# Output product by Strassen's algorithm over pairs of token blocks, in a mixer layer on one core

## The chip, the core and the metric

One core of a Trainium2 chip runs the whole layer in one launch. The metric is the device time of a run in microseconds (us); the time of a kernel is the median of its runs.

## What is computed

One layer of a mixer over 4096 tokens of width 1024, all in float32. The last product, `y @ W_out`, is the part that is changed.

```python
ada = cond @ w_ada[l] + b_ada[l]
shift, scale, gate = jnp.split(ada, 3, axis=-1)
h = _rms(x) * norm_gain[l]
h = h * (1.0 + scale[:, None, :]) + shift[:, None, :]
proj = h @ w_in[l]
q, k, v, g_attn, u, v_gm, g_gm = jnp.split(proj, splits, axis=-1)
attn = _windowed_gqa(q, k, v, q_gain[l], k_gain[l], sink[l])
gm = _chunked_gmlp(u, v_gm, w_s[l], b_s[l])
y = jnp.concatenate([attn * jax.nn.silu(g_attn), gm * jax.nn.silu(g_gm)], axis=-1)
x = x + gate[:, None, :] * (y @ w_out[l])
```

`x` is (1, 4096, 1024), `w_in` (1024, 2816), `w_out` (1024, 1024).

## The kernel before

The tokens are worked on in 32 blocks of 128 (`NB`), and widths in chunks of 128 (`KC` = 8). Every large product is made in three passes: each float32 operand is split into a high part (a cast to float32r on ACT) and a low part (the difference, on DVE or POOL), and high x high, high x low and low x high are added up in a bank of PSUM. So a group of 512 output columns over 1024 inputs takes 8 x 3 = 24 matmuls of 512 columns (`proj_ops`, L83).

There are three stages. The first makes q, k, v and the attention gate of each block and the windowed attention; the attention half of y goes to DRAM transposed (`yT[b][0]`). The second, the gMLP stage (loop at L905), makes v, g and u of each block (`gmlp_v`, `gmlp_gu`, `gmlp_u`; steps v and g of a block, block after block), 24 matmuls each, and after every four blocks the spatial mixing `gmlp_mix` (L839): 24 matmuls of 256 columns, evacuations on DVE, 16 transposes on PE, copies on ACT, and a store to `yT[b][1]`. In it, after blocks 8 to 17, the gate is made (`bg_gate`, `end_gate`).

The third stage makes the output. For each block `load3` (L958) loads the block of y and of x, `split3` (L966) splits y, and two groups of 24 matmuls follow, each evacuated by `out_block` (L976), which adds x on DVE and stores. The weights are loaded by `load_wo` (L882, multiplied by the gate on DVE or, for the last two rows, POOL) and split by `split_wo` (L887) from the last two blocks of the gMLP stage on; block 0 takes the weight rows one after the other as they are ready (loop at L985). Blocks 1 to 31 then run with all weights in SBUF (loop at L1002).

The pool `base` holds tiles over all stages, `hp` those of one stage (h2, then h3), `vr` (w2v) lies at the other end of SBUF and holds the weights of v and the buffers `raw2` (3). `y_tile` (L954) puts two of three blocks' operands into `base` and the third into the pool of the stage:

```python
    def y_tile(b, dt, tag, name):
        pool, bufs = (base, 2) if b % 3 < 2 else (hp, 1)
```

The Tile framework reorders instructions within an engine's queue by its own costs; every queue then runs in the order built. SP issues nearly all DMAs, in one queue.

Of the kernel before, what the change touches and what calls it, by code (L numbers as in the profile page):

```python
# [42 lines left out]
def body(tc, x, xT, c, cT, w_adaT, b_adaT, w_gate, b_gate, ngT, w_in, q_gain, k_gain, sink, wsT, bsT, w_out, out):  # L43
# [6 lines left out]
    yT = [[dram.tile([P, 4, P], F32, name=f"yT{b}_{h}") for h in range(2)] for b in range(NB)]  # L50

# [827 lines left out]
    woraw, woh2 = {}, []  # L879
    wo = [None] * KC  # L880

    def load_wo(k):  # L882
        woraw[k] = vr.tile([P, D], F32, tag="raw2", name=f"woraw{k}", bufs=3)
        nc.sync.dma_start(woraw[k], w_out[k * P : (k + 1) * P])
        (V if k < 6 else G).tensor_mul(woraw[k], woraw[k], gate)

    def split_wo(k):  # L887
        raw = woraw[k]
        if k < KC // 2:
            wo[k] = [[base.tile([P, 512], F32R, tag=f"{t}{2 * k + i}", name=f"wo{t}{k}_{i}") for i in range(2)] for t in "hl"]  # L890
        else:
            if not woh2:
                woh2.extend(halves("wo"))
            t = woh2[4 * k - 16 : 4 * k - 12]
            wo[k] = [t[:2], t[2:]]
        for i in range(2):
            r = raw[:, i * 512 : (i + 1) * 512]
            h, l = wo[k][0][i], wo[k][1][i]
            A.copy(h, r)
            V.tensor_tensor(l, r, h.bitcast(F32), ALU.subtract)  # L900
# [4 lines left out]
    for b0 in range(0, NB, NC):  # L905
# [19 lines left out]
        else:  # L925
            steps = [(n, b) for b in range(b0, b0 + NC) for n in "vg"]
        steps.append(("v", b0 + NC))
        for (n, b), (_, nb) in zip(steps[:-1], steps[1:]):
            if nb != b and nb < NB and (n, b) != ("u", 2):
                split2(nb)  # L930
            if n == "v":
                gmlp_v(b, vh, vl)
                continue
# [8 lines left out]
            if NB - 2 <= b:  # L942
                load_wo(b - (NB - 2))
# [6 lines left out]
    xp = p3.enter_context(tc.tile_pool(name="x3", bufs=4, reuse_waits="tile"))  # L950

    ld = {}

    def y_tile(b, dt, tag, name):  # L954
        pool, bufs = (base, 2) if b % 3 < 2 else (hp, 1)
        return pool.tile([P, KC, P], dt, tag=tag, name=f"{name}{b}", bufs=bufs)

    def load3(b):  # L958
        yr = y_tile(b, F32, "xraw", "yr")
        for h in range(2):  # L960
            nc.sync.dma_start(yr[:, 4 * h : 4 * h + 4], yT[b][h])
# [4 lines left out]
    def split3(b):  # L966
        yr, _ = ld[b]
        yh, yl = y_tile(b, F32R, "xh", "yh"), y_tile(b, F32R, "xl", "yl")
        A.copy(yh, yr)  # L969
        V.tensor_tensor(yl, yr, yh.bitcast(F32), ALU.subtract)  # L970
        return yh, yl

    woh = [[None] * KC for _ in range(2)]
    wol = [[None] * KC for _ in range(2)]

    def out_block(b, group, i):  # L976
        _, xt = ld[b]
        V.tensor_tensor(xt[:, i * 512 : (i + 1) * 512], group, xt[:, i * 512 : (i + 1) * 512], ALU.add)  # L978
        nc.sync.dma_start(out[b * P : (b + 1) * P, i * 512 : (i + 1) * 512], xt[:, i * 512 : (i + 1) * 512])

    NF = 1
    first = []
    for b in range(NF):
        load3(b)
    for k in range(KC):  # L985
        split_wo(k)
        if k + 2 < KC:
            load_wo(k + 2)
        for i in range(2):
            woh[i][k], wol[i][k] = wo[k][0][i], wo[k][1][i]  # L990
        if k == 0:
            for b in range(NF):
                yh, yl = split3(b)
                for i in range(2):
# [59 lines left out]
```

## Time and profile before

| | us |
|---|---|
| runs (3): median | 1760.36 |
| runs: lowest, highest | 1754.94, 1763.99 |
| profiled execution: its own time | 1755.96 |
| profiled execution: its span | 1754.2 |
| of it: first stage and start, to about | 860 |
| gMLP stage | 860 to 1391 |
| output stage | 1391 to 1754 |

The span runs from the first to the last instruction of one execution; 1.8 us lie around it. PE is TensorE's matmuls, PEld its weight loads, DVE VectorE, ACT ScalarE, POOL GpSimd, SP the engine that issues DMAs.

### The profile page before, as it was taken

How to read it: one execution, taken by the hardware profiler on the slowest of the kernel's cores; microseconds unless marked ns; L12 is line 12 of the kernel's file. 1: busy time of each engine (PE TensorE's matmuls, PEld its weight loads, DVE VectorE, ACT ScalarE, POOL GpSimd, SP SyncE). 2: the span in 40 equal slices, each digit the busy share in tenths (PEclk: the TensorE clock that was granted, in tenths of full speed). 3: DMA queues.
4: the chain of work that ended last, by engine and by line, in shares of the span. 5: the costliest groups of instructions: out<-in, count | busy, mean ns of one | idle time of the engine just before them, and what ended most of it. 6: DMA issues, size and time to landing. Idle time of an engine off the chain costs nothing.

```text
span 1754.2 us, 22761 instructions
## 1 busy us (share of the span) xinstructions
PE 1695.0 (97%) x8408; PEld 1405.0 (80%) x8408; DVE 988.4 (56%) x2143; ACT 689.8 (39%) x1505; POOL 522.7 (30%) x494
## 2 busy tenths in 40 slices
PE   6799999999999999998999999999999999999999
PEld 4578888888888888866778888888888788888887
DVE  7878787777888777779763332342333632222221
ACT  3476666666666666665511121212212310000000
POOL 5653334344333434356322222222232200000000
PEclk9899999999999999999999999999999999999999
DMA  7522221222221122123340111111111274444431
GB/s 261 186 84 72 73 67 48 68 73 73 73 73 61 49 72 91 37 66 109 98 151 27 59 50 36 49 38 59 49 36 49 85 231 144 143 145 144 143 131 60
DMA packets 61712, 156.24 MB, mean 89 GB/s; under 512 B 7584, under 2 KB 7584, under 8 KB 61600
## 3 DMA queue, kind: packets, MB, share of 16 engines
q1 hardware_dynamic: 56848, 146.13, 24.6%
q10 hardware_dynamic: 4752, 8.65, 1.3%
q8 instruction: 66, 1.08, 0.3%
q14 instruction: 46, 0.38, 0.1%
HBM read 121.20 MB, written 33.55 MB: 88 GB/s over the span
## 4 chain that ended last, share of the span: by engine, by line
PE 78%; DVE 10%; issue 2%; ACT 2%; POOL 1%; DMA 1%; SPq 0%; ACTq 0%; POOLq 0%; DVEq 0%
PE po L59 23%; PE pg L59 16%; PE pv L59 9%; PE pq L59 8%; PE pu L59 8%; PE pT L62 4%; PE s L59 4%; DVE y L598 2%; DVE pr L549 1%; PE sv L59 1%; PE pk L59 1%; DVE gf L493 1%; DVE qT L517 1%; ACT lo L596 1%; PE yT L62 1%
## 5 line engine op out<-in xcount | busy, mean ns | idle before, releaser
L95 POOL TENSOR_TENSOR xl<-xraw,xh 128x1024 fp32r<-128x1024 f32 x58 | 151.5, 2613 | 379.1 <-ACT xh L94 379.1
L569 POOL TENSOR_SCALAR pr<-pr,den 128x384 f32<-128x384 f32 (+1 forms) x256 | 147.2, 595 | 160.6 <-DVE vs L443 96.1
L978 DVE TENSOR_TENSOR xt<-po,xt 128x512 f32<-128x512 f32 x64 | 44.2, 691 | 254.2 <-PE po L59 251.4
L553 ACT ACTIVATE pr<-pr,mx 128x384 f32<-128x384 f32 (+1 forms) x256 | 153.8, 601 | 59.0 <-DVE mx L549 58.4
L59 PE MATMUL po<-wo,yh 128*128 128x512 f32 x512 | 158.9, 391 | 0.0
L549 DVE CUSTOM_DVE_ANT_0 pr<-s,negd,nsink 128x384 f32<-128x384 f32 (+1 forms) x256 | 152.2, 605 | 11.3 <-PE s L59 5.9
L578 ACT CAST ph<-pT 128x512 fp32r<-128x512 f32 x188 | 109.7, 585 | 116.5 <-PE po L59 44.2
L59 PE MATMUL pu<-w2u,xh 128*128 128x512 f32 x480 | 148.7, 391 | 0.0
L59 PE MATMUL s<-kT,qT 128*128 128x384 f32 (+1 forms) x512 | 135.6, 346 | 12.9 <-DVE mx L549 11.7
L969 ACT CAST yh<-yr 128x1024 fp32r<-128x1024 f32 x32 | 33.7, 1053 | 281.2 <-PE po L59 263.2
L579 DVE TENSOR_TENSOR pl<-pT,ph 128x512 fp32r<-128x512 f32 x188 | 125.9, 684 | 15.7 <-ACT ph L578 15.6
L62 PEld LDWEIGHTS pT<-ident,pr 128*128 128x128 f32 x752 | 93.6, 141 | 34.8 <-POOL pr L569 6.6
L62 PE MATMUL pT<-ident,pr 128*128 128x128 f32 x752 | 116.2, 274 | 5.2 <-DVE pl L579 3.4
L59 PEld LDWEIGHTS po<-wo,yh 128*128 128x128 f32 x512 | 96.3, 188 | 21.5 <-DVE wo L900 0.8
L59 PEld LDWEIGHTS s<-kT,qT 128*128 128x128 f32 x512 | 86.2, 188 | 33.5 <-DVE mx L549 20.6
L81 POOL TENSOR_TENSOR ssv<-ssv,mhalf 128x8 f32<-128x8 f32 x32 | 52.8, 1651 | 180.7 <-DVE ssv L80 180.5
L59 PEld LDWEIGHTS pu<-w2u,xh 128*128 128x128 f32 x480 | 90.8, 189 | 19.0
L94 ACT CAST xh<-xraw 128x1024 fp32r<-128x1024 f32 x61 | 64.1, 1051 | 101.4 <-PE pu L59 99.3
L59 PE MATMUL po<-woh,yh 128*128 128x512 f32 x256 | 100.3, 392 | 0.0
L59 PE MATMUL po<-wol,yh 128*128 128x512 f32 x256 | 100.2, 392 | 0.0
L59 PE MATMUL po<-wo,yl 128*128 128x512 f32 x256 | 100.1, 391 | 0.0
L59 PE MATMUL po<-woh,yl 128*128 128x512 f32 x256 | 100.0, 391 | 0.0
(288 smaller groups left out, 4302.0 us busy)
## 6 DMA issues: line engine op xcount, KB each, us to landing
xraw<-xT SPq DMA_DIRECT2D x61, 512.0 KB, 3.9
xtok<-x SPq DMA_DIRECT2D x32, 512.0 KB, 5.1
yr<-yT SPq DMA_DIRECT2D x64, 256.0 KB, 2.9
xt<-x SPq DMA_DIRECT2D x32, 512.0 KB, 4.7
out<-xt SPq DMA_DIRECT2D x64, 256.0 KB, 2.1
wada<-w_adaT SPq DMA_DIRECT2D x16, 512.0 KB, 5.6
yT<-ybuf ACTq DMA_DIRECT2D x32, 256.0 KB, 2.0
yT<-y SPq DMA_DIRECT2D x31, 256.0 KB, 5.2
```

What stands on the lines that cost most here:

```text
L59: pe(T.matmul(ps, lhsT, rhs, start=start, stop=stop))
L62: pe(T.transpose(ps, src, ident))
L81: G.tensor_tensor(dst, dst, mhalf[:, :width], ALU.pow)
L94: A.copy(xh, xr)
L95: ins = eng.tensor_tensor(xl, xr, xh.bitcast(F32), ALU.subtract)
L549: V.tensor_tensor_reduce(flat(t[:, s0:s1]), flat(pss[:, s0:s1]), flat(negd[:, b % 3, s0:s1]), -(2.0 ** -(h + 1)), nsink[:, h : h + 1], ALU ...
L553: A.activation(t, t, AF.Exp, bias=m[:, i : i + 1], scale=-1.0, accum_out=d["den", j][:, i : i + 1])
L569: G.tensor_scalar(t, t, den[:, i : i + 1], 1.0, ALU.mult, ALU.mult)
L578: A.copy(ph, pt)
L579: V.tensor_tensor(pl, pt, ph.bitcast(F32), ALU.subtract)
L598: V.tensor_tensor(d["y"][e * HD : (e + 1) * HD, 2 * j : 2 * j + 2], po[:HD, e::2], lo[:, e::2], ALU.add)
L978: V.tensor_tensor(xt[:, i * 512 : (i + 1) * 512], group, xt[:, i * 512 : (i + 1) * 512], ALU.add)
```

## The change

Two blocks of tokens are taken together. Their y is cut into four quarters A11, A12, A21, A22 (block i, half h of the 1024 inputs), the gated weights into B11, B12, B21, B22 (half of the inputs, half of the outputs). Seven products of halves take the place of eight, with four sums of quarters of y (S1 to S4, on POOL), four of the weights (T1 to T4, on DVE) and sums of the products, part of which PE makes by adding into the same bank (X, Y, Z). The weights and their sums are made once, in the gMLP stage (`wo_rows`, `wo_sums`, `wo_last`), stored in DRAM (`wB`), loaded again in pieces of 512 KB (`stage_w`) and split (`split_wm`): B11 and T2 into the place of v's weights, T3 and T1 into that of g's, the others when the output stage begins (`ready`). For this g of block 30 and v of block 31 change places. The first two products stand ahead of the last `gmlp_mix`.

```diff
+    wB = {m: dram.tile([P, KC // 2, 512], F32, name=f"wB_{m}") for m in ("B11", "T2", "T3", "T1", "B21", "B22", "T4")}
...
+    def wo_rows(k):
+        chunk["r"] = []
+        for kk in (k, k + KC // 2):
+            t = vr.tile([P, D], F32, tag="raw2", name=f"woraw{kk}", bufs=3)
+            nc.sync.dma_start(t, w_out[kk * P : (kk + 1) * P])
+            V.tensor_mul(t, t, gate)
...
+        V.tensor_tensor(t1, b12, b11, ALU.subtract)
+        V.tensor_tensor(t2, b22, t1, ALU.subtract)
+        V.tensor_tensor(b12, b22, b12, ALU.subtract)
+        for m, src in (("B11", b11), ("T1", t1), ("T2", t2), ("T3", b12), ("B21", b21), ("B22", b22)):
+            nc.sync.dma_start(wB[m][:, k], src)
...
+    ORDER = (("A11", "B11", "X"), ("S2", "T2", "Y"), ("S3", "T3", "Z"), ("S1", "T1", "Y"), ("A12", "B21", "X"),
+             ("S4", "B22", "Y"), ("A22", "T4", "Z"))
...
+    def split_wm(m, i, eng=None):
+        t = staged.pop((m, i))
+        for j in range(2):
+            h, l = (wts[m][a][2 * i + j] for a in range(2))
+            A.copy(h, t[:, j])
+            (eng or V).tensor_tensor(l, t[:, j], h.bitcast(F32), ALU.subtract)
...
+            G.tensor_tensor(sums3[n], q[a], q[b], op)
...
+    def prep3(p, i):
+        n = ORDER[i][0]
+        src = (quarters(p) | sums3)[n]
+        h, l = opnd[n]
+        A.copy(flat(h), src)
+        V.tensor_tensor(flat(l), src, flat(h).bitcast(F32), ALU.subtract)
...
+        for k in range(KC // 2):
+            for j, (l, r) in enumerate(((xh, wh), (xh, wl), (xl, wh))):
+                pe(T.matmul(ps, l[:, k], r[k], start=i < 3 and k == 0 and j == 0, stop=k == KC // 2 - 1 and j == 2,
+                            skip_group_check=i >= 3))
...
+        if i == 0:
+            A.copy(p1, banks["X"])
+        if i == 1:
+            V.tensor_tensor(u2, banks["Y"], p1, ALU.add)
+        if i == 3:
+            V.tensor_tensor(u4, banks["Y"], p1, ALU.add)
...
+        if i == 0:
+            G.tensor_tensor(x12, x12, part["p1"], ALU.add)
+        if i == 1:
+            G.tensor_tensor(x21, x21, part["u2"], ALU.add)
+        if i == 3:
+            G.tensor_tensor(x22, x22, ybuf[0], ALU.add)
...
+        if z:
+            V.tensor_tensor(dst, banks[z], dst, ALU.add)
...
+            nc.sync.dma_start(out[r0 : r0 + P, h * 512 : (h + 1) * 512], dst)
...
+            if b0 + NC == NB:
+                steps[5], steps[6] = steps[6], steps[5]
...
+    def ready(m):
         for i in range(2):
...
+            split_wm(m, i, (V, G)[i])
+            if pend:
+                stage_w(*pend.pop(0), hp, "stage", 3)
...
+            if p == 0:
+                if 1 <= i < 4:
+                    ready(late[i])
...
+            elif p + 1 < NP:
+                prep3(p + 1, i)
```

How the built order moves, at two places. PE, before, at the end of block 0 of the output stage (`po3_0_0`, `po3_0_1` are its two banks, `wo10` to `wo13` the high and low parts of the last weight row, `yh0`, `yl0` the split block):

```order
L59 MATMUL po3_0_0_13349<-wo10_13418,yh0_13345 128x512 [waits Activation_49]
L59 MATMUL po3_0_0_13349<-wo12_13420,yh0_13345 128x512 [waits DVE_49]
L59 MATMUL po3_0_0_13349<-wo10_13418,yl0_13346 128x512
L59 MATMUL po3_0_1_13350<-wo11_13419,yh0_13345 128x512 [waits Activation_49]
L59 MATMUL po3_0_1_13350<-wo13_13421,yh0_13345 128x512 [waits DVE_49]
L59 MATMUL po3_0_1_13350<-wo11_13419,yl0_13346 128x512
```

PE, now, in the first pair, behind the last transposes (`oX0`, `oY0`, `oZ0` are the banks of pair 0, `oX1` of pair 1; `woT1h`, `woT1l` are T1's parts, `wo0` to `wo5` B21's, `oxh1`, `oxl0`, `oA11` split operands):

```order
L967 MATMUL oY0_13428<-woT1l2_13407,oxh1_13410 128x512 [waits Pool_49]
L967 MATMUL oY0_13428<-woT1h2_13403,oxh1_13410 128x512
L967 MATMUL oY0_13428<-woT1h3_13404,oxh1_13410 128x512 [waits Activation_49]
L967 MATMUL oY0_13428<-woT1l3_13408,oxh1_13410 128x512 [waits Pool_49]
L967 MATMUL oY0_13428<-woT1h3_13404,oxh1_13410 128x512
L967 MATMUL oX0_13427<-wo0_13531,oxl0_13411 128x512 [waits Activation_49]
L967 MATMUL oX0_13427<-wo4_13535,oxl0_13411 128x512 [waits DVE_49]
L967 MATMUL oX0_13427<-wo0_13531,oxl0_13411 128x512
L967 MATMUL oX0_13427<-wo1_13532,oxl0_13411 128x512 [waits Activation_49]
L967 MATMUL oX0_13427<-wo4_13535,oxl0_13411 128x512 [waits DVE_49]
L967 MATMUL oX0_13427<-wo1_13532,oxl0_13411 128x512
L967 MATMUL oX1_13714<-wo3h0_13221,oA11_13250 128x512 [waits Activation_49]
```

PE now waits for POOL too, where the weights' low parts are split between DVE and POOL, and takes up pair 1 in the middle of pair 0.

POOL, before, its last work (the split and the norms of the last v blocks, then two weight rows; nothing follows):

```order
L95 TENSOR_TENSOR xl31_13103<-xraw31_13100,xh31_13102 128x1024 [waits DMAHW4_49,PE_49,Activation_49]
L81 TENSOR_TENSOR ssv30_13093<-ssv30_13093,mhalf_126 128x8 [waits DVE_49]
L81 TENSOR_TENSOR ssv31_13193<-ssv31_13193,mhalf_126 128x8 [waits DVE_49]
L885 TENSOR_TENSOR woraw6_13426<-woraw6_13426,gate_10659 128x1024 [waits DMAHW5_49,DMAHW7_49,DMAHW2_49,DVE_49]
L885 TENSOR_TENSOR woraw7_13439<-woraw7_13439,gate_10659 128x1024 [waits DMAHW6_49,DMAHW3_49,DVE_49]
```

POOL, now, from the second half of T1 on (`xt3_0` and `xt3_1` are x tiles, `s12` holds S1 and S2, `yr` and `yr3` are loaded blocks of y):

```order
L928 TENSOR_TENSOR woT1l2_13407<-stT1_1_13547,woT1h2_13403 128x512 [waits DMAHW4_49,PE_49,Activation_49]
L928 TENSOR_TENSOR woT1l3_13408<-stT1_1_13547,woT1h3_13404 128x512 [waits PE_49,Activation_49]
L984 TENSOR_TENSOR xt3_00_13526<-xt3_00_13526,p1_13253 128x512 [waits DMAHW6_49,DVE_49,PE_49]
L986 TENSOR_TENSOR xt3_01_13527<-xt3_01_13527,u2_13254 128x512 [waits DMAHW7_49]
L988 TENSOR_TENSOR xt3_01_13527<-xt3_01_13527,ybuf0_9850 128x512 [waits DVE_49]
L949 TENSOR_TENSOR S3_13389<-yr3_0_13524,yr3_1_13525 128x512 [waits DMAHW2_49,DMAHW0_49,Pool_49]
L949 TENSOR_TENSOR s12_13249<-yr3_1_13525 128x512 [waits DMAHW3_49]
L949 TENSOR_TENSOR s12_13249<-s12_13249,yr3_0_13524 128x512 [waits Pool_49]
L949 TENSOR_TENSOR S3_13389<-yr0_13237,yr1_13238 128x512 [waits DMAHW5_49,DVE_49]
L949 TENSOR_TENSOR S4_13390<-yr3_0_13524,s12_13249 128x512 [waits DMAHW1_49,Pool_49]
L928 TENSOR_TENSOR wo5_13536<-stB21_1_13568,wo2_13533 128x512 [waits DMAHW4_49,Activation_49]
L928 TENSOR_TENSOR wo5_13536<-stB21_1_13568,wo3_13534 128x512 [waits Activation_49]
```

POOL had no work in the output stage but for its start; now the additions to x, the sums of the next pairs and half of the weights' low parts stand in one queue.

## Rows read from the trace of the kernel before

**Rows 1.** The page, engine totals: busy us, share of the span, instructions.
```profile
PE 1695.0 (97%) x8408; PEld 1405.0 (80%) x8408; DVE 988.4 (56%) x2143; ACT 689.8 (39%) x1505; POOL 522.7 (30%) x494
```
**Rows 2.** Stages: us, busy PE, PEld, DVE, ACT, POOL, PEclk, DMA share, GB/s.
```profile
860.00:1391.00 531.00, 524.90 (x2410) 430.33 (x2409) 206.80 (x322) 110.41 (x159) 131.04 (x59) 1.00 0.17 59
1391.00:1410.00 19.00, 16.99 (x91) 13.40 (x90) 15.18 (x24) 8.34 (x15) 6.31 (x2) 1.00 0.52 174
1410.00:1750.00 340.00, 340.00 (x1489) 279.49 (x1488) 80.05 (x93) 31.59 (x30) 0.00 (x0) 1.00 0.42 141
```
**Rows 3.** The page, costliest groups: the output matmuls, count, busy us, mean ns.
```profile
L59 PE MATMUL po<-wo,yh 128*128 128x512 f32 x512 | 158.9, 391 | 0.0
...
L59 PE MATMUL po<-woh,yh 128*128 128x512 f32 x256 | 100.3, 392 | 0.0
L59 PE MATMUL po<-wol,yh 128*128 128x512 f32 x256 | 100.2, 392 | 0.0
L59 PE MATMUL po<-wo,yl 128*128 128x512 f32 x256 | 100.1, 391 | 0.0
L59 PE MATMUL po<-woh,yl 128*128 128x512 f32 x256 | 100.0, 391 | 0.0
```
**Rows 4.** The chain of waits, output stage: start us, us, what.
```profile
1402.59 1.01 PE yT L62 x8
...
1409.49 340.91 PE po L59 x1490
```
**Rows 5.** Timeline of PE, first matmuls of groups: start us, us, what.
```profile
1374.93 0.39 PE L59 MATMUL pv<-w2vh,xh 128*128 128x512 f32 x1
...
1380.53 0.39 PE L59 MATMUL pg<-w2gh,xh 128*128 128x512 f32 x1
...
1385.99 0.62 PE L59 MATMUL pu<-w2u,xh 128*128 128x512 f32 x2
...
1391.43 0.28 PE L59 MATMUL sv<-vh,wsh 128*128 128x256 f32 x1
...
1392.85 0.39 PE L59 MATMUL po<-woh,yh 128*128 128x512 f32 x1
```
**Rows 6.** Timeline of PE, first matmuls of output blocks 2, 3 and 4.
```profile
1420.96 0.40 PE L59 MATMUL po<-woh,yh 128*128 128x512 f32 x1
...
1432.12 0.39 PE L59 MATMUL po<-woh,yh 128*128 128x512 f32 x1
...
1443.00 0.39 PE L59 MATMUL po<-woh,yh 128*128 128x512 f32 x1
```
**Rows 7.** Groups by line and form: count | busy us, mean ns | idle before.
```profile
L777 POOL TENSOR_TENSOR w2vl<-w2rawv,w2vh 128x512 fp32r<-128x512 f32 x4 | 5.2, 1290 | 9.4 <-PE po L59 7.9 <-ACT w2vh L776 1.5
...
L900 DVE TENSOR_TENSOR wol<-woraw,woh 128x512 fp32r<-128x512 f32 x8 | 5.3, 685 | 0.6 <-ACT woh L899 0.6
...
L899 ACT CAST woh<-woraw 128x512 fp32r<-128x512 f32 x8 | 4.7, 618 | 6.1 <-PE pg L59 5.4 <-DVE woraw L885 0.6
```
**Rows 8.** Timelines of POOL and DVE, start of the output stage.
```profile
1396.75 2.39 POOL L885 TENSOR_TENSOR woraw<-woraw,gate 128x1024 f32<-128x1024 f32 x1 [10.62 <-DMA woraw<-w_out]
1403.14 3.92 POOL L885 TENSOR_TENSOR woraw<-woraw,gate 128x1024 f32<-128x1024 f32 x1 [4.00 <-DVE wo L900]
...
1397.87 1.81 DVE L900 TENSOR_TENSOR wo<-woraw,wo 128x512 fp32r<-128x512 f32 x1
```
**Rows 9.** DMA issues (count, KB each, us to landing), and a stage as in rows 2.
```profile
woraw<-w_out SPq DMA_DIRECT2D x8, 512.0 KB, 3.3
...
1410.00:1420.00 10.00, 10.00 (x45) 8.26 (x45) 4.25 (x5) 2.10 (x2) 0.00 (x0) 1.00 0.91 300
```
**Rows 10.** Timeline of POOL: the split of block 31.
```profile
1359.57 2.85 POOL L95 TENSOR_TENSOR xl<-xraw,xh 128x1024 fp32r<-128x1024 f32 x1 [7.73 <-ACT xh L94]
```
**Rows 11.** Two stretches of the first stage, columns as in rows 2.
```profile
60.00:70.00 10.00, 4.78 (x24) 3.41 (x22) 9.93 (x13) 1.51 (x3) 5.42 (x3) 0.99 0.58 211
70.00:80.00 10.00, 6.94 (x17) 3.84 (x18) 8.69 (x19) 8.52 (x19) 8.00 (x8) 0.67 0.28 106
```

More of the change, by code (lines that the diff above doesn't have):

```diff
@@ L877, in end_gate @@
             V.tensor_tensor(gate[:, cs], ps, w[:, cs], ALU.add)
[L879 to L895, printed above, removed]
-        for i in range(2):
[L897 to L900, printed above, removed]
+    chunk = {}
@@ new lines, in wo_last, with stage_w @@
+    def wo_last(k):
+        b21, t2 = chunk["t4"]
+        V.tensor_tensor(b21, b21, t2, ALU.subtract)
+        nc.sync.dma_start(wB["T4"][:, k], b21)
+    SUMS = ("S1", "S2", "S3", "S4")
+    ORDER = (("A11", "B11", "X"), ("S2", "T2", "Y"), ("S3", "T3", "Z"), ("S1", "T1", "Y"), ("A12", "B21", "X"),
+             ("S4", "B22", "Y"), ("A22", "T4", "Z"))
+    NP = NB // 2
+    wts, staged, raw3, opnd, sums3, xt3, banks, part = {}, {}, {}, {}, {}, {}, {}, {}
+    def stage_w(m, i, pool, tag, bufs):
+        t = pool.tile([P, 2, 512], F32, tag=tag, name=f"st{m}_{i}", bufs=bufs)
+        nc.sync.dma_start(t, wB[m][:, 2 * i : 2 * i + 2])
+        staged[m, i] = t
@@ new lines, in quarters, with sum3 @@
+    def quarters(p):
+        r = raw3[p % 2]
+        return {f"A{i + 1}{h + 1}": flat(r[i][:, 4 * h : 4 * h + 4]) for i in range(2) for h in range(2)}
+    def sum3(p, names):
+        q = quarters(p) | sums3
+        for n in names:
+            a, b, op = {"S1": ("A21", "A22", ALU.add), "S2": ("S1", "A11", ALU.subtract),
+                        "S3": ("A11", "A21", ALU.subtract), "S4": ("A12", "S2", ALU.subtract)}[n]
+            G.tensor_tensor(sums3[n], q[a], q[b], op)
[5 more added lines that the diff above has]
+        V.tensor_tensor(flat(l), src, flat(h).bitcast(F32), ALU.subtract)
@@ new lines, in before_last2, with behind_last @@
+    def before_last2():
+        split_wm("B11", 0)
+        split_wm("B11", 1)
+        sum3(0, ("S1", "S2"))
+        prep3(0, 0)
+        stage_w("T2", 1, vr, "raw2", 3)
+        split_wm("T2", 0)
+        split_wm("T2", 1)
+        prep3(0, 1)
+    def behind_last():
+        sums3.update((n, base.tile([P, 512], F32, tag="bgw", name=n, bufs=2)) for n in ("S3", "S4"))
+        sum3(0, ("S3", "S4"))
+        for i, m in enumerate(("T3", "T1")):
+            wts[m] = [[base.tile([P, 512], F32R, tag=f"{t}{4 * i + k}", name=f"wo{m}{t}{k}") for k in range(4)] for t in "hl"]
+        xx = [base.tile([P, 2, 4, P], F32R, tag=t, name=f"o{t}{i}", bufs=2) for t in ("xh", "xl") for i in range(2)]
+        for n, o in zip(("S3", "S1", "A12", "S4"), xx):
+            opnd[n] = o[:, 0], o[:, 1]
+        for i in range(2):
+            stage_w("T3", i, vr, "raw2", 3)
+            split_wm("T3", i)
+        prep3(0, 2)
+        prod3(0, 0)
+        post3(0, 0)
+        prod3(0, 1)
+        post3(0, 1)
@@ L966, in split3 @@
[L966 to L979, printed above, removed]
@@ L1000, in body @@
[L1000 to L1010 removed]
+    raw3[1] = [hp.tile([P, KC, P], F32, name=f"yr3_{i}") for i in range(2)]
+    for q in range(2):
+        xt3[q] = [hp.tile([P, D], F32, name=f"xt3_{q}{i}") for i in range(2)]
@@ new lines, in body @@
+    o = hp.tile([P, 2, 4, P], F32R, name="oA22")
+    opnd["A22"] = o[:, 0], o[:, 1]
+    hv = halves("wo")
+    wts["B21"], wts["B22"] = w_tiles(hv[:8]), w_tiles(hv[8:])
+    late = ("T1", "B21", "B22", "T4")
+    stages = [(m, i) for m in late for i in range(2)]
+    for m, i in stages[:3]:
+        stage_w(m, i, hp, "stage", 3)
+    load_x3(0)
+    load3(1)
+    pend = stages[3:]
+    def ready(m):
+        for i in range(2):
+            split_wm(m, i, (V, G)[i])
+            if pend:
+                stage_w(*pend.pop(0), hp, "stage", 3)
```

129 lines of the change are left out of this document (85 added, 44 removed).

## The prediction

> **What bounds the kernel now.** I read the profile from the whole to the stretch that is changed. The engine totals come first: PE is busy 97% of the span, the next engine 56% [rows 1]. The table by stage then shows where this holds without a gap: from 1410 to 1750 us, the output product, PE is busy 340.0 of 340.0 us at a granted clock of 1.00, with DVE at 80, ACT at 32 and POOL at 0; in the gMLP stage before it PE has 525 of 531 us and DVE 207 [rows 2]. The chain of waits says the same: its last piece but the drain is 340.9 us of output matmuls, one behind the other [rows 4]. So the end is set by the number of matmuls times their pitch, and whatever takes matmuls out of this stage shortens the kernel, as long as no feeder becomes late. The groups give the count, 512 and four times 256, or 1536 matmuls of 512 columns [rows 3]. Their 391 ns is an overlapped duration; the pitch is the distance of starts, and it depends on where the operands lie. A block of 48 takes 11.16 us where its operand tile is in the pool of the stage (every third block) and 10.88 us where all operands are in the pool base [rows 6]: 0.2325 against 0.2267 us. The gMLP stage agrees: 24 matmuls whose weights lie in w2v take 5.60 us, 24 with weights in base 5.46, both with an operand tile in base [rows 5].
>
> **The change, part by part.**
>
> *Matmuls.* Each pair of blocks takes seven products of 12 matmuls, 84 where two blocks took 96; 16 pairs take 1344, 192 fewer. Before: ten blocks at 11.16 and 22 at 10.88 make 351.0 us. Afterwards I sort the products by where their operands lie. Four (S3, S1, A12, S4) are all in base: 48 x 0.2267 = 10.88. A11 with B11 has one operand outside: 12 x 0.2333 = 2.80. S2 with T2, and A22 with T4, have both outside. Both outside is seen only in the 12 spatial matmuls of 256 columns, 0.118 us each (1.42 us for 12 [rows 5]), so I take 0.236 for 512 columns: 24 x 0.236 = 5.66. A pair is 19.34 us and 16 pairs 309.5: **41.5 us less**. The bounds are 46 (all at 0.2267) and 40 (24 at 0.240).
>
> *The steady pair.* I let the elementwise work cost nothing, covered by the 19.3 us of matmuls of a pair. DVE has 13 operations of 0.69 (7 low parts, 2 partial results, 4 output adds), 9.0 us; ACT 8 of 0.62, 5.0; POOL 7 of 1.29, 9.0 [rows 7]. The output adds and products use banks that alternate from pair to pair. The one tight chain is inside a pair: the second group in bank Z may only start when DVE has read the first, and that read waits for POOL to add u4 to the x tile. From the end of the fourth product this is 0.69 + 1.29 + 0.69, some 2.7 us, and two products, 5.5 us, lie between. Loads are 2 MB and stores 1 MB a pair, 163 GB/s, where the stage before ran bursts at 300 [rows 9].
>
> *The start of the stage.* Before, from the first spatial matmul of the last four blocks (1391.43 [rows 5]) to the unbroken run (1409.49 [rows 4]) 18.1 us pass. Their work is 24 spatial matmuls (2.8), 16 transposes at 0.126 (2.0, from eight in 1.01 [rows 4]) and 46 output matmuls (10.5), so 2.7 us are lost there now. In the changed order the first two products stand ahead of the spatial matmuls and cover DVE's work on them; I leave 1.5 us for that piece. The new cost comes behind the last transpose. The tile that takes T1's second half lies over the gMLP output tile, so its load starts only there: 3.3 us [rows 9] and a cast of 0.62, 4 us. From then on POOL must do 17 operations up to the last low part of T4 (two each for T1, B21, B22, T4; the rest are x additions and sums): 17 x 1.29 = 21.9 us. PE has 85 matmuls up to T4's last, 19.5 us, so at least 4 + 21.9 - 19.5 = 6 us are lost. DVE has 15 operations with two SBUF inputs in the same stretch, 10.3 us. The trace shows what two such operations do to each other: a DVE subtraction that began inside a POOL multiplication of 2.39 us took 1.81 us instead of 0.69 and ended 0.54 us behind POOL's end [rows 7, 8]. If all 15 keep POOL out, the stretch is 4 + 32.2 us and 17 us are lost. The loads give the same lower end: 6 MB up to T4 at 300 GB/s are 20 us, and behind them a cast and two POOL operations. [...] I take 12, since some of DVE's operations fall where POOL waits for a load or for PE. With the 1.5 the start loses 13.5 us where it lost 2.7: **10.8 us more** (bounds 3.7 and 17).
>
> *Weight sums in the gMLP stage.* Eight multiplications (two of 0.69 in length) and 16 additions or subtractions of 0.69 give DVE 22 us, which the built order puts into blocks 18 to 20. Eight of the 24, the multiplications, were in the start of the output stage before. DVE has 324 us free in the gMLP stage [rows 2], so this is covered, except at one place: the multiplication of the chunk's row 3 stands between two spatial evacuations of block group 16, and may wait there for its load of 3.3 us while PE waits for the evacuation. The 28 stores of 256 KB go past the loads of x blocks on SP's queue; those are issued over 20 us ahead. I take **1 us** (0 to 4).
>
> *The exchange of g30 and v31.* The split of block 31 must now be done while PE works on v30, 5.6 us: cast about 1.2 and POOL 2.85 [rows 7, 10], 4.1 us. Nothing.
>
> *Tail.* As before: one DVE addition and one store.
>
> **Sum.** -41.5 + 10.8 + 1 = -29.7 us. The profiled execution is 1755.96 us, so 1726.3; its time lies 4.4 us under the median of the runs, from which the same sum gives 1730.7. I put **1728 us**, and with the bounds of the terms 1713 to 1741.
>
> **The rivals.**
>
> *The start costs almost nothing.* If DVE and POOL interleave and PE finds the products of the second pair ready, the loss stays under 4 us and the time is about 1717. For: PE's order already holds pieces of the second pair between those of the first. Against: these pieces need sums that stand in the same POOL queue. Chance 0.18.
>
> *The clock falls in the start.* PE would have some 20 us of work in 33. In the first stage a stretch with PE busy 4.8 of 10 us was followed by one at a granted clock of 0.67 [rows 11]; from 1391 to 1410, busy 17 of 19, it stayed at 1.00 [rows 2]. At 0.67 over the stretch, 19.5 us of matmuls become 29, up to 9.5 us more: 1738. [...] Chance 0.14.
>
> *POOL becomes the bound of every pair: slower.* POOL has 7 additions a pair. If each took 2.75 us, POOL would need PE's 19.3 us; at 3.2 us a pair is 22.4 us, sixteen pairs lose 49 us against the forecast, and the time is 1777. For: POOL's multiplication of 1024 columns took up to 3.92 us beside DVE [rows 8], 1.96 for half the size, and each of DVE's 7 low parts can hold it off for 0.69. Against: 1.96 is under 2.75, and even 1.29 plus 0.69 is. It decides from 2.75 us on. Chance 0.06.
>
> *Small stalls in every pair* (about 2 us, by the tight chain above when POOL is in the middle of the next sum): 1758, no change. Chance 0.06. That the change does not do what it says is excluded: the built order holds 1344 output matmuls.
>
> **How the numbers follow.** The forecast, 1728, has 0.56. Range 1713 to 1746: it takes in the cheap start, the fallen clock with 8 us for the median's offset and the bounds, and leaves the last two rivals out. Half a percent, 8.8 us, is about what a measurement of this kernel can tell from no change. Faster by more: 0.88 (the first three cases). Within it: 0.06. Slower: 0.06.
>
> **What would show it.** Right: two blocks' worth of output in 19.2 to 19.5 us from the third pair on with PE at ten tenths; in the first some 35 us behind the last transpose PE near 60%, with waits put down to POOL's low parts of B21, B22 and T4. Wrong: steady pairs over 20 us, with Z's second group waiting for DVE; or a start in which PE is dense; or a granted clock under 1.00 there.

## The result and the profile after

The changed kernel takes **1737.2 us** (median of 4 runs, 1734.84 to 1738.58) where the kernel before takes 1760.0 (4 runs, 1754.94 to 1763.99): 22.8 us less, a ratio of 0.987 (95% interval 0.984 to 0.990). The forecast was 1728, with a range from 1713 to 1746. The profiled execution took 1734.84 us (span 1733.1), 21.1 us under that of before, and this difference can be split along the program. Forecast and measurement, in us against the profiled execution before:

| term of the forecast | forecast | measured | how |
|---|---|---|---|
| Matmuls | -41.5 | -43.0 | 16 pairs of 19.25 (308.0) instead of 351.0 |
| The start of the stage | +10.8 | +13.7 | 59.77 from the end of the last projection to the third pair, less two pairs (38.51) and the spatial matmuls and transposes (4.85), is 16.4; before 2.7 |
| Weight sums in the gMLP stage | +1 | +7.0 | 28.5 instead of 21.4 from u of block 19 to u of block 20 |
| Exchange, pairs' elementwise work, tail | 0 | 0 | what is left over |
| ahead of all that (first mix of the gMLP stage) | | +1.2 | u of block 4, the first behind that mix, at 910.35 instead of 909.19 |
| sum | -29.7 | -21.1 | |

So the saving came as worked out, and 9 us more than forecast were given back at two places. The page's engine totals of the kernel after, which answer to [rows 1]:

```profile
PE 1659.0 (96%) x8216; PEld 1370.8 (79%) x8216; DVE 1069.3 (62%) x2277; ACT 739.2 (43%) x1613; POOL 690.9 (40%) x612
```

PE has 192 matmuls fewer, and its busy time falls by 36 us and not by 43, since stretches with waits or a lower clock count as busy for longer (48.9 us in the start, below, for 43.3 of work); POOL has 168 us more. By stage, with the columns of [rows 2]: the gMLP stage with the first two products, the rest of the start, and the steady pairs.

```profile
860.00:1410.00 550.00, 538.72 (x2467) 441.48 (x2466) 238.34 (x363) 115.93 (x170) 137.08 (x63) 0.99 0.24 81
1410.00:1460.00 50.00, 39.47 (x155) 28.01 (x155) 29.95 (x33) 20.32 (x36) 33.45 (x24) 0.97 0.69 238
1460.00:1730.00 270.00, 269.15 (x1175) 220.07 (x1173) 115.40 (x177) 63.49 (x106) 135.83 (x93) 1.00 0.47 153
```

The third row is as dense as the output stage before (the last matmul ends at 1729.2), with POOL at half its time. PE's timeline gives the pair: the first product of the third, the fourth and the last pair, and the last product.

```profile
1459.45 0.39 PE L967 MATMUL oX<-wo3h,oA 128*128 128x512 f32 x1
...
1478.70 0.39 PE L967 MATMUL oX<-wo3h,oA 128*128 128x512 f32 x1
...
1709.74 0.39 PE L967 MATMUL oX<-wo3h,oA 128*128 128x512 f32 x1
...
1726.22 0.40 PE L967 MATMUL oZ<-woT,oA 128*128 128x512 f32 x1
```

The first and the second are 19.25 apart, and the 13 pairs from the first to the third row make 250.29 us, 19.25 each. Where the start loses time is in PE's waits from 1399 to 1460 (total, count, longest):

```profile
PE oX L967 <- DVE oA L956: 2.6, 1, 2.6
PE oX L967 <- POOL wo L928: 2.3, 2, 1.6
PE oY L967 <- ACT woT1h L927: 2.1, 2, 1.2
PE oY L967 <- POOL woT1l L928: 1.1, 2, 0.9
PE oX L967 <- ACT oA L955: 1.1, 1, 1.1
PE oY L967 <- POOL wo L928: 0.7, 2, 0.4
```

These and smaller ones make 10.9 of the 16.4 us. Of the rest, a granted clock of 0.66 from 1427 to 1432 accounts for some 1.7 (an estimate: 5 x 0.34); what else slows PE there was not found. POOL's timeline shows what part of the waits rests on: it can start only when T1's second half has landed and is cast, 5.8 us behind the last transpose (1412.1), and is then in work with one break until B21's low parts are made (1436.5). T4's low parts end its row at 1446.7.

```profile
1417.89 2.51 POOL L928 TENSOR_TENSOR woT1l<-stT,woT1h 128x512 fp32r<-128x512 f32 x2 [14.53 <-ACT woT1h L927]
1421.14 1.58 POOL L984 TENSOR_TENSOR xt<-xt,p 128x512 f32<-128x512 f32 x1 [0.74 <-DMA xt<-x]
...
1431.41 1.74 POOL L949 TENSOR_TENSOR S<-yr,s 128x512 f32<-128x512 f32 x1
1433.11 3.40 POOL L928 TENSOR_TENSOR wo<-stB,wo 128x512 fp32r<-128x512 f32 x2
...
1443.86 2.85 POOL L928 TENSOR_TENSOR woT<-stT,woT 128x512 fp32r<-128x512 f32 x2 [1.60 <-ACT woT L927]
```

The other place is the mixing of blocks 16 to 19. In the kernel before PE is busy 50.00 of 50.00 us from 1160 to 1210 (first row); after, it is not (second row), and behind the gap it has a lower clock (third row; columns as above):

```profile
1160.00:1210.00 50.00, 50.00 (x239) 41.14 (x238) 17.25 (x30) 10.45 (x15) 13.47 (x6) 1.00 0.15 53
...
1160.00:1210.00 50.00, 45.11 (x208) 36.58 (x207) 33.48 (x46) 9.69 (x14) 9.27 (x5) 0.97 0.70 234
...
1188.00:1193.00 5.00, 4.71 (x23) 4.11 (x24) 3.41 (x8) 0.00 (x0) 0.00 (x0) 0.66 0.70 277
```

DVE's timeline there, behind the u matmuls that end at 1179.9 (start us, us, what, idle before it):

```profile
1171.05 0.69 DVE L245 TENSOR_REDUCE ssv<-sqv 128x8 f32<-128x512 f32 x1 [0.76 <-ACT sqv L243]
1175.76 1.23 DVE L891 TENSOR_TENSOR woraw<-woraw,gate 128x1024 f32<-128x1024 f32 x1 [4.03 <-DMA woraw<-w_out]
...
1183.71 0.69 DVE L909 TENSOR_TENSOR woraw<-woraw,wosum 128x512 f32<-128x512 f32 x1 [0.18 <-DMA wB_B<-woraw]
1184.32 0.74 DVE L830 SCALAR_TENSOR_TENSOR ug<-pu,rstd,bias 128x512 f32<-128x512 f32 x1
1185.17 1.99 DVE L831 TENSOR_TENSOR ug<-ug,gfm 128x512 f32<-128x512 f32 x1
1187.27 1.66 DVE L851 SCALAR_TENSOR_TENSOR ug<-sv,bs,ug 128x256 f32<-128x256 f32 x4
```

In the kernel before, where those matmuls end at 1178.65, the same three steps (its lines 828, 829 and 849) are

```profile
1178.85 0.75 DVE L828 SCALAR_TENSOR_TENSOR ug<-pu,rstd,bias 128x512 f32<-128x512 f32 x1 [4.02 <-PE pu L59]
1179.70 0.69 DVE L829 TENSOR_TENSOR ug<-ug,gfm 128x512 f32<-128x512 f32 x1
1180.50 1.66 DVE L849 SCALAR_TENSOR_TENSOR ug<-sv,bs,ug 128x256 f32<-128x256 f32 x4
```

After the change DVE stands 4.03 us for a chunk's load, with the norm of block 19 and the sums of that chunk behind it. So L830 starts 4.4 us behind the u matmuls instead of 0.2. By then POOL's split (2.60 us from 1184.02) has begun, which before began just behind the start of the gate product; now the gate product L831 starts beside it and takes 1.99 instead of 0.69. The evacuations L851 start 7.4 us behind the u matmuls instead of 1.9: 5.5 us late, 4.2 of them because DVE is late and 1.3 because POOL holds L831 off. PE waits for them:

```profile
1188.29 0.36 PE L61 MATMUL sv<-vh,wsh 128*128 128x256 f32 x1 [3.60 <-DVE ug L851]
...
1189.89 0.41 PE L61 MATMUL sv<-vl,wsh 128*128 128x256 f32 x1
1190.11 0.41 PE L61 MATMUL sv<-vh,wsl 128*128 128x256 f32 x1
```

The last two are 0.22 apart, where spatial matmuls stood 0.118 apart before. PE's idle time in this mix is 4.9 us: 3.60, and 0.70 and 0.59 ahead of it for the split of v, which stands behind the late norm. The lower clock takes most of the remaining 2.1.

### The profile page after: what moved, and what is told of

Same layout as the page of the kernel before. It is cut to its first block, busy times and chain, and to the rows that moved or that the text cites. A ratio compares the mean times of both kernels' runs of the same rounds, so it can differ in the third digit from the quotient of the medians.

```text
span 1733.1 us, 23001 instructions
## 1 busy us (share of the span) xinstructions
PE 1659.0 (96%) x8216; PEld 1370.8 (79%) x8216; DVE 1069.3 (62%) x2277; ACT 739.2 (43%) x1613; POOL 690.9 (40%) x612
## 4 chain that ended last, share of the span: by engine, by line
PE 78%; DVE 10%; ACT 2%; DMA 1%; issue 1%; POOL 1%; SPq 0%; POOLq 0%; DVEq 0%; ACTq 0%
PE pg L61 17%; PE pv L61 9%; PE pu L61 9%; PE pq L61 9%; PE oY L967 7%; PE oX L967 5%; PE oZ L967 5%; PE pT L64 5%; PE s L61 5%; PE po L61 3%; DVE y L600 2%; DVE pr L551 1%; PE sv L61 1%; PE pk L61 1%; DVE gf L495 1%
## 5 line engine op out<-in xcount | busy, mean ns | idle before, releaser
L61 PE MATMUL pg<-wgh,xl 128*128 128x512 f32 x232 | 98.4, 424 | 0.0
L61 PE MATMUL pg<-wgh,xh 128*128 128x512 f32 x232 | 98.2, 423 | 0.0
L61 PE MATMUL pu<-w2u,xl 128*128 128x512 f32 x240 | 94.3, 393 | 1.2 <-DVE xl L97 1.2
L61 PE MATMUL pq<-w1h,xh 128*128 128x512 f32 x232 | 94.1, 406 | 0.0
L61 PE MATMUL pq<-w1l,xh 128*128 128x512 f32 x232 | 93.8, 404 | 0.0
L61 PE MATMUL pq<-w1h,xl 128*128 128x512 f32 x232 | 91.9, 396 | 0.0
L61 PE MATMUL pg<-wgl,xh 128*128 128x512 f32 x232 | 91.5, 395 | 0.0
L61 PE MATMUL pv<-w2vh,xh 128*128 128x512 f32 x224 | 90.7, 405 | 0.0
```

Of the source, the lines that this page charges most:

```text
L61: pe(T.matmul(ps, lhsT, rhs, start=start, stop=stop))
```

## The experiments

Single runs of one kernel differ by some us in the stages ahead of the change, so stretches of the profile are compared besides the times: the mixes by the distance from one u projection to the next (21.4 us across a mix in the kernel before), the start by the distance from the last u matmul to the third pair's first product. Five kernels whose start is untouched give 59.6 to 61.9 us for the latter (the changed kernel 60.0, counted from the start of that matmul and so 0.2 more than in the table), so about a microsecond either way says nothing. The kernel before took 1757.6 to 1758.7 us (medians of 7 to 9 runs) beside the variants and 1760.0 beside the changed kernel, so medians of different kernels are good to 1 or 2 us.

### Where the weight sums stand

**The sums pinned to the program's order.** Each operation of `wo_rows`, `wo_sums` and `wo_last` goes behind what is written ahead of it on DVE:

```diff
-            V.tensor_mul(t, t, gate)
+            tc.keep_in_program_order(V.tensor_mul(t, t, gate))
```

> The weight sums are kept where the program has them: each chunk's two multiplications behind block 18, 21, 24 or 27, its three sums one block later, its last sum two blocks later; loads, stores and operation counts are as in the changed kernel. Theory 1 (the place): the 8.3 us by which the last gMLP projection ends later (1399.7 instead of 1391.4) come from the built order packing four chunks into blocks 18 to 20, where DVE's queue stands 4.0 us for a w_out load and the evacuations of block group 16 come late. Then the stretch from 1160 to 1210 is dense again at a granted clock of 1.00, the projection ends at 1391 to 1393, and the time is 6.5 to 8.5 us shorter, about 1730 us. Rival (the traffic): 4 MB of loads and 7.3 MB of stores through the queue of the x blocks delay those; spread or not, most of the loss stays, and the time is 0 to 2 us shorter, about 1736 us.

Measured: 1735.4 us (4 runs; ratio 0.987, 0.986 to 0.989). No wait for a load is left and DMA is spread out, but the time is not shorter: across the mixes behind blocks 19, 23 and 27 it takes 23.6, 23.6 and 25.1 us, 7.9 us lost in place of 7.0. The traffic rival had the time right, but the losses stand at three points and nowhere else, which traffic does not explain. So this run takes away the late queue of the changed kernel and puts another cost in its place: right behind the gate product of the last block of four there now stands a sum (blocks 19 and 23) or two multiplications (block 27). DVE and POOL behind block 23:

```profile
1253.90 0.69 DVE L831 TENSOR_TENSOR ug<-ug,gfm 128x512 f32<-128x512 f32 x1
1254.51 2.87 DVE L909 TENSOR_TENSOR woraw<-woraw,wosum 128x512 f32<-128x512 f32 x1
```

```profile
1253.99 2.85 POOL L97 TENSOR_TENSOR xl<-xraw,xh 128x1024 fp32r<-128x1024 f32 x1 [7.73 <-ACT xh L96]
```

A sum of 0.69 us takes 2.87: it started inside POOL's split and ended 0.54 us behind it, the figure of [rows 8]; the expectations below call such a hold the lock. PE waits 2.03 us for the evacuations behind it. Not every such hold cost PE: in the changed kernel the sum L902 at 1164.69 took 2.88 us beside POOL's split of 2.48, away from a mix, and PE had no gap.

**The sums clear of the mixes.** Four sums in one step, the last into a tile of its own; steps at blocks that are not the last of four:

```diff
+    SLOTS = (18, 20, 21, 22, 24, 25, 26, 28)
...
-            if 18 <= b < 30:
-                (wo_rows, wo_sums, wo_last)[b % 3]((b - 18) // 3)
+            if b in SLOTS:
+                n = SLOTS.index(b)
+                (wo_rows, wo_sums)[n % 2](n // 2)
```

> As the run that pins the sums, but no sum or multiplication stands behind the last block of a group of four, where DVE's evacuations of the spatial matmuls are due: multiplications behind blocks 18, 21, 24, 26, all four sums of a chunk behind 20, 22, 25, 28 (the last sum into a tile of its own). Same loads, stores and operations. Theory 1b (the lock at the mix): what costs is one operation with two SBUF inputs that starts beside POOL's 2.85 us split just ahead of the evacuations, 2.0 to 2.1 us of PE at each of three mixes in the pinned run; without one there all mixes are as in the kernel before, the 7.2 us (in the pinned run 7.9 us) are gone, and the time is 6 to 8 us shorter than the changed kernel's, about 1729 us. Rival (the traffic): the loss stays at 4 us or more wherever the sums stand, and the time is 0 to 3 us shorter.

Measured: 1731.2 us (5 runs; ratio 0.984, 0.983 to 0.986), span 1727.4. The three mixes take 21.4, 21.5 and 21.4 us, as before the change, with the same loads, stores and DVE operations. The stretch that had 45.11 us of PE:

```profile
1160.00:1210.00 50.00, 50.00 (x238) 41.19 (x237) 25.25 (x34) 10.28 (x15) 11.83 (x5) 1.00 0.21 74
```

So all of the 7.0 us was the place of the operations, not their number and not their transfers. How much of it was the wait for the load and how much POOL's hold, no run separates; the changed kernel's own timeline gives the 4.2 and 1.3 us above.

**A probe of three operations** in the version just described:

```diff
+            if b in (19, 23, 27):
+                a, c = gate[:, :256], gate[:, 256:512]
+                if b == 19:
+                    ins = V.tensor_tensor(spare[0], a, c, ALU.subtract)
+                elif b == 23:
+                    ins = V.tensor_scalar_mul(spare[0], a, scolg[:, 0:1])
+                else:
+                    ins = V.scalar_tensor_tensor(spare[0], a, scolg[:, 0:1], c, ALU.mult, ALU.add)
+                tc.keep_in_program_order(ins)
```

> The version with the sums clear of the mixes, and one small DVE operation of 256 columns (some 0.3 us, its result is not used) right behind the last gate product of block 19, 23 and 27, where POOL is in its 2.85 us split and the evacuations are due: at 19 a subtraction of two SBUF operands, at 23 a multiplication of one SBUF operand by a column, at 27 the fused multiply-add of two SBUF operands and a column. Theory 1b (an operation with two SBUF inputs waits until POOL's operation ends): the ones at 19 and 27 take 2.2 to 2.9 us and cost PE about 2 us each, the one at 23 takes 0.3 us and costs PE nothing or at most 0.3 us. Rival (any DVE operation in that place delays the evacuations, by its own length): all three take 0.3 us and PE waits less than 0.5 us at each. Second rival (every SBUF operation is held off, with one input too): all three take over 2 us.

Measured, by the operations that touch the gate's tile (`spare` is a part of it; count, ns, start):

```profile
L1095 DVE TENSOR_TENSOR gate<-gate x1: 2600/2600/2600, 1184.3 to 1184.3; 128x256 f32<-128x256 f32 x1
L1097 DVE TENSOR_SCALAR gate<-gate,scolg x1: 2458/2458/2458, 1258.7 to 1258.7; 128x256 f32<-128x256 f32 x1
L1099 DVE SCALAR_TENSOR_TENSOR gate<-gate,scolg x1: 2601/2601/2601, 1331.8 to 1331.8; 128x256 f32<-128x256 f32 x1
```

PE waits 1.99, 2.08 and 1.99 us, and the mixes take 24.9, 23.6 and 25.0. My expectation was right for two inputs and wrong for one: the operation with a single SBUF input was held off as well, as the second rival had it, and took 2.46 us for 256 columns, where a multiplication by a column of the kernel before, with POOL idle, took 0.75 us for 1024 (its L866, at 864.96). One form of it was tried. L830, which reads PSUM, was not held off: in the changed kernel's timeline above it took 0.74 us inside POOL's split, and 0.75 in the kernel before (its L828), ahead of the split.

### What sets the start

**POOL's low parts to DVE**, and, by itself, **POOL's x additions and sums to DVE** (first pair's additions, second pair's sums):

```diff
-            split_wm(m, i, (V, G)[i])
+            split_wm(m, i)
```

```diff
+        E = G if p else V
...
-            G.tensor_tensor(x12, x12, part["p1"], ALU.add)
+            E.tensor_tensor(x12, x12, part["p1"], ALU.add)
...
-                    sum3(1, SUMS)
+                    sum3(1, SUMS, V)
```

> The eight low parts of T1, B21, B22 and T4 that POOL makes in the start of the output stage are made by DVE; nothing else. Theory 2 (POOL's queue): PE waits in the start because B21's low parts stand behind eight x additions and sums on POOL (1421.1 to 1433.1) and everything behind them is late; without them in that queue the start is 3 to 6 us shorter, about 1732 us. Rival (the loads): the transfers run at 390 to 410 GB/s from 1417 to 1427 and set when anything can start; then the time moves by less than 1 us. Second rival (DVE's queue): DVE stands behind an output addition that waits for POOL, and eight more operations of 0.69 us there make it 0 to 4 us longer, about 1739 us.

> The other half of POOL's work in the start goes to DVE: the three x additions of the first pair and the four sums of the second; the eight low parts stay on POOL. Theory 2 (POOL's queue): B21's low parts no longer stand behind them, 8 x 1.3 us leave POOL's queue, and the time is 3 to 6 us shorter, about 1732 us; the wait of the second pair's first product for the low part of A11 (2.6 us) goes too. Rival (the loads): less than 1 us. If this gains and the move of the low parts does not, what counts is the place in the queue and not how much POOL has to do.

Measured: 1738.0 us (4 runs) with a start of 59.7, and 1734.2 (4 runs) with 58.1. By the start, neither gained the 3 to 6 us of the theory of POOL's queue alone: 0.3 and 1.9. (The median of the second lies 3.0 us under the changed kernel's, but its ratio to the kernel before, 0.987, is the changed kernel's.) With the low parts on DVE, PE's waits fell from 10.9 to 8.6 us, but the granted clock was 0.51 from 1420 to 1425 (1.00 in the changed kernel) and PE's busy time in the start rose from 48.9 to 50.8 us, so the gain went.

**T1 staged early**, where T2 and T3 were staged before it:

```diff
+        for i in range(2):
+            stage_w("T1", i, vr, "raw2", 3)
         prep3(0, 2)
...
-    stages = [(m, i) for m in late for i in range(2)]
+    stages = [(m, i) for m in late[1:] for i in range(2)]
```

> T1 is staged where T2 and T3 were staged before it, so both its loads are issued during the last block's projections instead of behind the last transposes, and the three staging tiles of the output stage begin with B21. Theory 3 (the late load, the first 4 us of the term of the start): the fourth product follows the third without its 3.5 us of waits, the 1 MB of T1 is no longer in the crowd behind 1412, and the time is 3 to 5 us shorter, about 1733 us. Rival (POOL's queue sets the end of the start): what is gained at T1 is lost again at B21, and the time is 0 to 1.5 us shorter.

Measured: 1734.1 us (4 runs; ratio 0.986), start 58.2, 1.8 less: between theory and rival. No wait for T1 is left, and what comes first now is B21:

```profile
PE oX L967 <- DVE wo L928: 4.2, 2, 3.5
PE oY L967 <- POOL wo L928: 1.6, 1, 1.6
PE oY L967 <- DVE oS2l L956: 1.2, 1, 1.2
```

The waits are 8.4 us instead of 10.9, and again part of it is paid in clock (two stretches of this run, columns as above):

```profile
1420.00:1430.00 10.00, 6.96 (x21) 5.06 (x22) 9.51 (x9) 3.10 (x6) 9.73 (x7) 0.83 1.03 394
1435.00:1445.00 10.00, 8.11 (x22) 5.66 (x23) 6.51 (x6) 2.72 (x6) 7.90 (x6) 0.66 0.10 39
```

**More transfers, more POOL work.** 2 MB from DRAM to DRAM ahead of the x tiles; four additions behind the second pair's sums:

```diff
+    for i in range(4):
+        tc.keep_in_program_order(nc.sync.dma_start(dram.tile([P, D], F32, name=f"extra{i}"), x[i * P : (i + 1) * P]))
     load_x3(0)
```

```diff
                     sum3(1, SUMS)
+                    for _ in range(4):
+                        tc.keep_in_program_order(G.tensor_tensor(ybuf[1], quarters(1)["A21"], quarters(1)["A22"], ALU.add))
```

> Adds 2 MB of transfers from DRAM to DRAM on SP's queue, ahead of the x tiles of the first pair, which nothing waits for; nothing else. Measured from the last projection matmul to the first product of the third pair: 60.0 us in the changed kernel. Theory 4 (the transfers set the end of the start, since moving POOL's work either way gained 0.3 and 1.9 us): 2 MB at 400 GB/s are 5 us, and the start is 4 to 6 us longer. Theory 2 (POOL's queue sets it): less than 1.5 us longer.

> Adds four additions of 128x512 to POOL's queue behind the sums of the second pair, ahead of B21's low parts; their result is not used. Measured as before, 60.0 us in the changed kernel. Theory 2 (POOL's queue): 4 x 1.29 = 5.2 us longer, 4 to 7 us with the lock. Theory 4 (the transfers): less than 1.5 us longer. If both this run and the one with more transfers are longer by most of what was added, the two form one chain: the load that POOL's operation waits for, and then POOL's queue.

Measured, one run each: starts of 68.4 and 64.0 us. Both lengthen the start, the transfers by 8.4 (more than the 5 of the expectation) and POOL's 5.2 us by 4.0. PE's waits make about half of it, 4.5 and 2.0 us; the rest went with a lower clock (0.67 from 1420 to 1440 with more transfers, 0.72 from 1420 to 1430 with more POOL work; 0.91 from 1420 to 1430 in the changed kernel), so by how much each link alone lengthens the start is not shown. With more transfers PE's longest wait is for A11 of the second pair (5.4 us, its cast waits for the load of y, which SP's queue issues from 1422.87 instead of 1414.22), with more POOL work for B21's low parts (3.8 us). So the two bear on different waits of PE, and both count, as the last sentence of the expectation has it: loads behind the last transposes, then POOL's queue, and PE behind both.

**The edits together**, and with them **half of B21 staged early** too (`stage_w("B21", 0, vr, "raw2", 3)` behind T1's; T4's tiles, which lie in the same buffers, are taken later for it):

> Three of the edits together: no sums at the mixes, T1 staged ahead of the last transposes, and the first pair's x additions and the second pair's sums on DVE. By theory 1b 6 to 8 us less in the gMLP stage; in the start the two edits gained 1.8 and 1.9 us apart: together 2 to 5 us if each shortens another wait, no more than 2 us if the transfers set its end. In all about 1726 us (1722 to 1730), the shortest of the versions.

> The combined version, with the first half of B21 also staged ahead of the last transposes. What PE waits for first in its start is the low part of B21 (3.3 us, its load comes behind the last transposes). If loads of the weights are what is late, 1 to 3 us less than the combined version, about 1725 us, and the third pair 54 to 56 us behind the last projection (56.7 there); if the crowd of transfers as a whole sets the end, 0 to 1 us.

Measured: 1727.6 us (4 runs; ratio 0.983, 0.981 to 0.984) with a start of 56.7, and **1725.0 us** (5 runs; ratio 0.981, 0.979 to 0.983) with 55.6. The last edit's own gain, 2.6 us in the medians and 1.1 in the start, is within the spread of either. The gains of the start add up (1.8 and 1.9 us alone; together 3.8, from 60.5 with the sums clear to 56.7), as they do when each shortens another link. The last version beats both kernels, 12 us under the change as it was made. Its start (55.6 us, of which the work is 43.3) is not dense either: PE still waits 2.6 us for DVE's partial result u2 and 1.9 for A11, and its clock is low once more:

```profile
1420.00:1430.00 10.00, 7.40 (x18) 5.03 (x19) 6.99 (x13) 3.81 (x7) 2.27 (x2) 0.66 0.96 377
```

### The terms put at nothing

**More POOL work in every pair**, seven subtractions of 256 columns from the third pair on:

```diff
+    junk = hp.tile([P, 256], F32, name="junk")
...
+                if p > 1:
+                    G.tensor_tensor(junk, part["p1"][:, :256], part["p1"][:, 256:], ALU.subtract)
```

> From the third pair on POOL makes seven more subtractions of 128x256 in every pair (their result is not used); in the built order they stand in one row behind the x addition of the first product. At half of 1.29 us each they are 4.5 us, so POOL has 14 to 16 us of work in a pair of 19.26 us. The forecast's reading (POOL has room, and the sums for the next pair and the addition of the fourth product still come in time): a pair stays at 19.26 to 19.3 us. The rival that let POOL bound every pair, or the small stalls of the chain inside a pair: a pair is longer by 0.5 to 4.5 us, the kernel by 7 to 60 us.

Measured, one run: from the fourth pair on PE is without a gap while POOL is busy about 80% (78 to 81 in the four stretches of 50 us from 1500):

```profile
1500.00:1550.00 50.00, 50.00 (x218) 40.51 (x217) 27.02 (x33) 12.65 (x21) 39.12 (x37) 1.00 0.53 180
```

Twelve pairs from 1480.76 to 1713.75 take 19.42 us each, 0.16 more than in the changed kernel and outside my 19.3, but as pitch and not as a wait: the last two products of a pair take 2.81 and 2.88 us instead of 2.73 and 2.77. The extra tile also moves other tiles of its pool, and which of the two does it was not tried. The third pair, the first with the added work, takes 20.56 us and has one wait:

```profile
1477.86 3.06 PE L967 MATMUL oZ<-woT,oA 128*128 128x512 f32 x12 [1.03 <-DVE xt L997]
```

That is the tight chain of the forecast: bank Z is read late, because DVE waits 4.39 us for POOL to add u4 to the x tile, and that addition stands behind the added row (6.76 us). So the rival of small stalls is real; with this much more on POOL it cost 1.0 us, once.

**The exchange undone**, in the version with the sums clear:

```diff
-            if b0 + NC == NB:
-                steps[5], steps[6] = steps[6], steps[5]
...
-            if b == NB - 2:
+            if b == NB - 1:
                 before_last2()
```

> The version with the sums clear of the mixes, with g30 and v31 in the old order again; the split of B11 and T2 and the first pair's operands then come behind block 31's gate instead of block 30's. From the first gMLP mark (the start of the third u projection) to the last projection 483.8 us and from there to the third pair's first product 60.5 us in the version with the exchange. The forecast put the exchange itself at 0; if what it buys (time for DVE to make the first two products' operands before PE is at the end of the gMLP stage) counts, undoing it makes the sum of the two stretches 2 to 6 us longer, with PE waiting for the last low parts of B11, T2 or S2; if DVE catches up in the last 11 us of projections anyway, less than 1 us.

Measured, one run: from the u projection of block 4 (the mark of the expectation) to the last one 476.7 us with and without it (the 483.8 of the expectation is the changed kernel's, with the sums where they were), no wait of PE ahead of the spatial matmuls, and a start of 61.6 instead of 60.5, inside the spread of untouched starts. DVE catches up in the last projections; a gain or loss of about 1 us stays open.

## Why the prediction was right, and where its terms were not

**What bounds the kernel** held: the end is set by matmuls times pitch, and the saving came nearly whole, in spite of 81 us more of DVE's work and 168 us more of POOL's.

**Matmuls** (-41.5, measured -43.0, inside its bounds of 46 and 40). The pitch with both operands outside `base` was set too high: S2 with T2 takes 2.75 us for 12 and A22 with T4 2.77, 0.229 and 0.231 each, where I took 0.236 from matmuls of half the columns. A11 with B11 takes the 2.80 of the forecast, so both outside is not dearer than one. S3 with T3, all in `base`, takes 2.76 where I took 2.72, so the pool alone does not fix the pitch.

**The steady pair** at no cost: right, and the rivals of small stalls and of POOL as the bound did not come true. A pair is 19.25 us without a gap, and with POOL loaded to about 80% only one wait of 1.0 us came, at the place that I had named as tight.

**The start** (+10.8, measured +13.7, inside 3.7 to 17; as a difference to before the upper end should have been 15.8, since the 17 is the loss behind the last transposes itself). The mechanism was right in the main: T1's late half, then POOL's queue with DVE's operations in between. The size I chose, 12 us behind the last transposes, was too small. POOL began 5.8 us behind them where I had 4, was busy 24.6 us with its 17 operations where I had 21.9, and stood idle for 4.2 us among them, which I had at nothing; 34.6 us less PE's 19.5 leave 15.1. So DVE held POOL off for some 3 us in all (an estimate from these sums), far from the 10.3 of the case in which all 15 of its operations keep POOL out. PE was busier than my sign of 60% (24.4 of 34.9 us behind the last transpose), and only 4.4 of its 10.9 us of waits are put down to POOL's low parts; the longest, 2.6, is for DVE's low part of A11. The rival of the fallen clock came true in part beside it: 0.66 from 1427 to 1432, not over the whole stretch. The runs show more than the forecast said: loads and POOL are links of one chain, so relief of one alone gained 0.3 to 1.9 us, and in two runs shorter waits went with a lower clock.

**Weight sums in the gMLP stage** (+1, bounds 0 to 4, measured +7.0) is the step that failed. I costed DVE's 22 us at nothing because DVE has 324 us free in the stage [rows 2], and named one exception, the multiplication of the last chunk between two evacuations, which may wait for its load. There DVE stood 1.59 us (before 1190.52; the profile does not say for what), and no matmul waited behind it. What cost was the same kind of wait at another place, which I had not looked for: 4.03 us at the multiplication of the chunk before, with the norm and the gate of block 19 behind it in the queue. Together with that chunk's sums it made the evacuations 4.2 us late, and so late that the gate product fell beside POOL's split, for 1.3 us more. I had the row for such a hold and used it for the start only: [rows 8], 1.81 us in place of 0.69. PE's waits came to 4.9 us, and the clock behind them took most of the other 2.1. The pinned run shows that the hold by itself is worth as much: without any wait for a load, one operation on SBUF operands in front of the evacuations of each mix made PE wait about 2 us, and the mix with a clock of 0.58 behind the wait (1333 to 1337) took 25.1 us where the other two, at 1.00, took 23.6.

The total stayed inside the range although this term left its bounds, because the bounds of the start are 13 us wide; that part of the forecast was luck. One reading of mine was wrong without effect: of the eight multiplications of the kernel before, three stood in the middle of the gMLP stage (1146.9 to 1152.6) and not in the start of the output stage.

**Ahead of the change** 1.2 us went that no term had: the first mix of the gMLP stage took 1.6 us more, and 0.4 was gained ahead of it; see the last section.

## What to carry to other kernels

Free time of an engine summed over a stage says nothing of an operation's place: in an in-order queue ask whether the operation itself may wait for a load, what stands right behind it, and whether PE waits for that (here DVE stood 4.03 us for one load, and PE 3.60 us for the evacuations behind it). Keep DVE operations on SBUF operands out of the stretches in which POOL works and DVE has evacuations due; here it was worth about 6 us to pin the same work behind other blocks, where it neither waited for its loads nor stood in front of evacuations. When a stage is entered through a chain of loads and elementwise work, lengthen each link in turn: if several answer, relief of one gains little (here 0.3 to 1.9 us), and relief of several together adds up (3.8).

## What the runs showed of the hardware

That the DVE operation with a single SBUF input was held off beside POOL's split I had not expected: it took 2.46 us for 256 columns and ended 0.16 us behind the split of 2.83 us; the two with two inputs took 2.60 and ended 0.28 us behind theirs, of 2.84.

The clock after equal waits differed. At the first mix of the gMLP stage both kernels wait 2.34 us for DVE, at the same place of the same order of PE. Behind it, the kernel before:

```profile
896.00:900.00 4.00, 3.70 (x26) 3.21 (x26) 2.68 (x7) 0.49 (x2) 0.00 (x0) 1.00 0.36 139
```

and the changed kernel:

```profile
896.00:900.00 4.00, 3.95 (x20) 3.94 (x21) 2.17 (x6) 0.00 (x0) 0.00 (x0) 0.60 0.36 122
```

At 0.60 from 896 to 900, and 0.50 from 896 to 899, PE makes 20 matmuls where it made 26. The same with the three operations placed at mixes: behind waits of 1.99, 2.08 and 1.99 us the clock was 0.72, 1.00 and 0.66 over 5 us (from 1187, 1261 and 1335). Across the first mix, from the u matmul ahead of it that waits 1.24 us (at 879.10 in the kernel before) to u of block 4, the kernel before takes 30.1 us; the changed kernel, the exchange undone, the last version of the start and the probe of three operations lose 1.5 to 1.7 us against it, and the run with more POOL work in every pair loses nothing. What decides it stays open.
